# Source order on every engine through the mixer and the attention of a hybrid decoder layer

## The chip, the cores and the metric

The kernel runs on one core of one Trainium2 chip. The metric is the device time of one execution in microseconds (us), from 3 runs of the kernel before: 849.39, 850.27 and 852.31, median 850.27. A core has five engines with a queue each: TensorE (PE in the profile, with its weight loads as PEld), VectorE (DVE), ScalarE (ACT), GpSimd (POOL) and SyncE (SP). The compiled program gives each engine a list of instructions in a fixed order; semaphores order the engines among each other. SP and POOL also issue the DMAs.

## The reference

One decoder layer in f32 over 512 positions of width 1024:

- RMSNorm, then one projection whose columns are cut into two head groups. The HGRN2 group (4 heads of 128) is a gated linear recurrence, computed in chunks of 32 positions: forget gates through a sigmoid, running products of them, a masked product inside a chunk, states from chunk to chunk, an RMSNorm per head and a swish gate. The MoBA group (4 heads of 128) is causal attention with partial rotary. With 512 positions there are two blocks of 256, so all past blocks are chosen and the result is plain causal softmax attention.
- The outputs of both groups side by side go through the output projection; residual add.
- RMSNorm, then cross-attention with 4 heads of 256 into 256 memory tokens, which have an RMSNorm of their own; residual add.
- RMSNorm, an MLP of width 4096 with the square of relu; residual add; a final RMSNorm.

```python
h = rms_norm(x, norm_mix);  hq, hf, hi, hg, mq, mk, mv = split(h @ w_in)
x = x + concat([hgrn2_mixer(hq, hf, hi, hg, ...), moba_attention(rot(mq), rot(mk), mv)]) @ w_out
x = x + cross_attention(rms_norm(x, norm_xattn), rms_norm(mem, norm_mem), w_xq, w_xk, w_xv, w_xo)
x = x + square(relu(rms_norm(x, norm_mlp) @ w_ff1)) @ w_ff2
return rms_norm(x, norm_final)
```

## The kernel before

**Numbers in two parts.** Every f32 operand of a large product is split in a high part in fp32r (ACT: a copy, `wh`) and a low part (DVE: a subtraction, `wl`). A product is three matmuls: high by high, high by low, low by high. The MLP's two products use a Strassen-like scheme with seven block products in place of eight.

**Units.** The weights are cut into units of 128 x 1024 f32 (512 KB). A unit of a projection is eight k steps of three matmuls of 512 columns, 24 matmuls; a unit of `memk` has 24 of 256 columns, one of `memv` 12 of 512. The mixer and the cross-attention are units 0 to 67, in this order: `hf` 4 units, `hi` 4, `hq` 4, `mv` 4, `mkq` 8 (keys and queries of MoBA in turn), `hg` 4, `wo` 8 (output projection), `memk` 8, `xq` 8, `memv` 8, `xo` 8. Then comes the MLP.

**Loads and splits.** `need(u)`, called ahead of the matmuls of unit u, emits the work for later units: the split of unit u+2 (`SPLIT_AHEAD`) and the load of about unit u+5, since at most three raw tiles wait for their split (`RAWS`; four in the MLP). There are four tiles for high and four for low parts (`WBUFS`). Each load also emits one or two DMAs of the sums of weight blocks that the Strassen scheme wants (`more_sums`): copies from DRAM to DRAM on SP's queue (line 202) and accumulating DMAs on POOL's queue (line 205). Each of these waits for the last matmul of an earlier unit.

**Side work.** Between the matmuls of the units stands side work: the HGRN heads (`hgrn_pre`, `hgrn_out`), the MoBA heads (`moba_head`), the norms, the preparation of the memory (`mem_prep`) and the heads of the cross-attention (`xattn_probs`, `xattn_out`). Each is a Python generator that is started by the evacuation of a unit and yields where it wants to wait. Counted in the source, `hgrn_out` has 7 steps with PE work per head, `moba_head` 10, the cross-attention 10; with four heads each that is 28 + 40 + 40 = 108.

**The planner.** `Pace` keeps an estimate of when each tile is ready, from costs written into `note`: PE runs strictly in the order of emission; DVE, ACT, POOL and the DMAs take an instruction into the first gap that is long enough. After at least `GAP` = 4 matmuls `pump` emits the next step of the first piece of side work whose inputs are ready, by the planner, `SLACK` = 2.5 us before PE's planned time. `drain` emits all that is left of a piece at once, where the next unit cannot do without it. All instructions go through the planner's call at line 115, so nearly all rows of the profile have L115.

**What sets the order.** The compiler has a scheduler of its own: outside a region that the kernel marks as ordered it chooses the order of each engine's instructions at compile time, by a simulated run with its own costs. Inside a region opened by `tc.manual_schedule()` each engine issues its instructions in the order in which the source emits them. The kernel before has two such regions: from the start to `lower_bounds()` behind `hf`'s third unit (closed at line 565), and from the MLP's first group (opened at line 1155) to the end. Between them, from unit 3 through `xo`, the scheduler orders. The kernel's last line of the layer, 1248, closes the second region.

**Memory.** PSUM has four banks for the accumulators of the units and four for side work (`side_bank`). SBUF has 12 large tiles (`s8`, 128 x 2048 f32), 14 small ones (`s2`, 128 x 512) and 8 more small ones for the mixer (`e2`).

Of the kernel before, what the change touches and what calls it, by code (L numbers as in the profile page):

```python
# [122 lines left out]
def hybrid_layer(ctx: ExitStack, tc: tile.TileContext, xT, memT, ws, vecs, consts, rots, out):  # L123
# [12 lines left out]
    ordered = tc.manual_schedule()  # L136
# [144 lines left out]
    def need(u):  # L281
        marks.append(last_mm[0])
        want_load, want_split = min(UNITS, u + LOAD_AHEAD + 1), min(UNITS, u + SPLIT_AHEAD + 1)
        while state["split"] < want_split or state["load"] < want_load:
            if state["load"] < want_load and state["load"] - state["split"] < RAWS + (u >= MLP):
                load_unit()
            elif state["split"] < want_split:
                split_unit()
            else:
                break  # L290
# [244 lines left out]
    def lower_bounds():  # L535
        l0, l1 = vec[:, V_LB:V_LB + 4], vec[:, V_LB + 4:V_LB + 8]
        V.tensor_max(lb, l0, l1)
        V.tensor_sub(le0, l0, lb)
        V.tensor_sub(le1, l1, lb)
        A.activation(lbv[:, 2:4, :], lbv[:, 2:4, :], AF.Exp)  # L540
        V.tensor_add(le1, le0, le1)
        V.reciprocal(le1, le1)
        V.tensor_mul(lb, le0, le1)
        V.tensor_scalar(oml, lb, -1.0, 1.0, op0=ALU.mult, op1=ALU.add)
# [17 lines left out]
        if k == NORM_AT:  # L562
            next(norm_x)
    lower_bounds()
    ordered.__exit__(None, None, None)
    need(3)
    for k in range(KT):
        fm_k(3, accs[3], x_act, k, k == 0, k == KT - 1)
# [583 lines left out]
        while op_state[0] < min(28, i + 1):  # L1152
            make_op()

    ordered = tc.manual_schedule()
    ordered.__enter__()
    for j in range(8):
        f1_group(j)
        u += 7
# [163 lines left out]
```

## Time and profile before

| | |
|---|---|
| median of 3 runs | 850.27 us (849.39 to 852.31) |
| the profiled execution | 853.37 us, its span 851.4 us, 2.0 us outside of it |
| mean granted TensorE clock | 0.954 |
| PE busy | 768.0 us, 90% of the span |
| DVE busy | 536.2 us, 63% |
| ACT busy | 412.2 us, 48% |
| POOL busy | 89.8 us, 11% |
| DMA | 165.87 MB, mean 195 GB/s |

The span runs from the first to the last instruction; the rest of an execution's time lies around it. "Idle before, releaser" in a row names the engine and tile that ended a wait. Tiles carry their names without numbers: `wh<-wr` is the high part of some unit's weights, `mkq<-xhi,wl` a matmul of the stage `mkq` with the low part of a unit's weights. The granted clock is the share of its full rate that the throttle left to TensorE.

### The profile page before, as it was taken

What the parts mean: (1) busy time and instruction counts of PE and PEld (TensorE: products, weight loads), DVE (VectorE), ACT (ScalarE), POOL (GpSimd) and SP (SyncE); (2) the same over time, 40 slices, a digit from 0 to 9 for tenths busy, and PEclk for the clock granted to TensorE, in tenths of its full rate; (3) what the DMA queues carried; (4) which work ended last, traced back from release to release, by engine and by line L of the source; (5) the groups of instructions that cost most, each with busy time, mean ns of one, the idle gap of its engine ahead of it and who ended that gap; (6) DMA issues with size and microseconds to landing.
All of it is one profiled execution on the core that took longest, in us unless ns stands there. A gap on an engine that the chain in (4) does not pass through costs nothing.

```text
span 851.4 us, 12049 instructions
## 1 busy us (share of the span) xinstructions
PE 768.0 (90%) x4696; PEld 680.1 (80%) x4696; DVE 536.2 (63%) x854; ACT 412.2 (48%) x633; POOL 89.8 (11%) x99
## 2 busy tenths in 40 slices
PE   6998769669997796799999999999999999999994
PEld 3787647447775686788888899999999899989994
DVE  6896540346754276447655775667676767867783
ACT  6652472022453255434445566555555654455662
POOL 5140002101001021100131001100000000110011
PEclk9999979878998997899999999999999999998998
DMA  7443219958518969995699569986555565995641
GB/s 243 155 143 123 75 34 295 192 97 222 149 50 207 317 179 302 243 355 200 168 264 269 164 216 258 246 268 190 185 184 179 168 200 168 242 261 157 211 161 50
DMA packets 57481, 165.87 MB, mean 195 GB/s; under 512 B 5424, under 2 KB 7856, under 8 KB 56656
## 3 DMA queue, kind: packets, MB, share of 16 engines
q1 hardware_dynamic: 43632, 131.09, 45.0%
q0 software_dynamic: 13312, 33.56, 21.9%
q8 instruction: 37, 0.61, 0.3%
q10 hardware_dynamic: 480, 0.45, 0.2%
q14 instruction: 20, 0.16, 0.1%
HBM read 162.98 MB, written 65.01 MB: 268 GB/s over the span
## 4 chain that ended last, share of the span: by engine, by line
PE 54%; issue 18%; DVE 13%; ACT 6%; DMA 6%; POOL 1%; SPq 0%; POOLq 0%; ACTq 0%; DVEq 0%
PE X L115 9%; PE xo L115 6%; PE mkq L115 6%; PE Y L115 5%; PE xq L115 5%; DVE wl L115 4%; PE memk L115 3%; PE wo L115 3%; PE mv L115 3%; PE hg L115 3%; PE memv L115 3%; DMA mraw<-in_memT_dram 2%; ACT wh L115 2%; PE hq L115 2%; ACT L115 2%
## 5 line engine op out<-in xcount | busy, mean ns | idle before, releaser
L115 DVE TENSOR_TENSOR wl<-wr,wh 128x1024 fp32r<-128x1024 f32 (+1 forms) x179 | 214.9, 1213 | 123.8 <-ACT wh L115 117.2
L115 ACT ACTIVATE wh<-wr 128x1024 fp32r<-128x1024 f32 (+2 forms) x182 | 185.3, 1040 | 112.1 <-DMA wr<-in_ws_dram 48.6
L115 PE MATMUL X<-op,wh 128*128 128x256 f32 x512 | 97.8, 292 | 4.0 <-DVE op L115 1.2
L115 PEld LDWEIGHTS X<-op,wh 128*128 128x128 f32 x512 | 83.4, 200 | 5.2 <-DVE op L115 1.6
L115 PE MATMUL X<-op,wl 128*128 128x256 f32 x256 | 74.8, 292 | 1.5 <-DVE wl L115 1.5
L205 POOL DMA_DIRECT2D uf<-in_ws_dram x32 | 26.2, 872 | 386.8 <-PE X L115 190.3
L115 PEld LDWEIGHTS X<-op,wl 128*128 128x128 f32 x256 | 51.0, 199 | 2.2 <-DVE wl L115 2.1
L205 POOL DMA_DIRECT2D ue<-in_ws_dram x32 | 28.8, 1000 | 227.0 <-PE mv L115 75.7
L115 PE MATMUL Y<-op,wh 128*128 128x256 f32 x256 | 46.7, 284 | 0.6 <-DVE op L115 0.6
L115 PE MATMUL X<-OS,wh 128*128 128x256 f32 x256 | 47.0, 283 | 0.0
L115 PE MATMUL Y<-OS,wh 128*128 128x256 f32 x256 | 46.8, 283 | 0.0
L115 ACT ACTIVATE op<-g 128x1024 fp32r<-128x1024 f32 x28 | 29.4, 1050 | 34.5 <-DVE g L115 34.5
L115 ACT ACTIVATE g<-t 128x512 f32<-128x512 f32 x32 | 19.4, 628 | 55.0 <-DVE t L115 54.9
L115 DVE TENSOR_TENSOR op<-g,op 128x1024 fp32r<-128x1024 f32 x28 | 34.2, 1222 | 16.7 <-ACT op L115 16.7
L115 PEld LDWEIGHTS Y<-op,wh 128*128 128x128 f32 x256 | 40.0, 192 | 1.0 <-DVE op L115 1.0
L115 PEld LDWEIGHTS X<-OS,wh 128*128 128x128 f32 x256 | 40.0, 192 | 0.0
L115 PEld LDWEIGHTS Y<-OS,wh 128*128 128x128 f32 x256 | 39.9, 192 | 0.0
L115 PE MATMUL X<-OS,wl 128*128 128x256 f32 x128 | 36.3, 284 | 0.6 <-DVE wl L115 0.6
L115 PE MATMUL Y<-OS,wl 128*128 128x256 f32 x128 | 36.2, 283 | 0.0
L115 PE MATMUL Y<-op,wl 128*128 128x256 f32 x128 | 36.2, 283 | 0.0
L115 PE MATMUL wo<-mixhi,wh 128*128 128x512 f32 x64 | 27.3, 427 | 9.6 <-DVE x L115 4.9
L115 PE MATMUL mkq<-xhi,wl 128*128 128x512 f32 x64 | 28.4, 444 | 4.8 <-DVE wl L115 4.8
(298 smaller groups left out, 2022.8 us busy)
## 6 DMA issues: line engine op xcount, KB each, us to landing
wr<-in_ws_dram SPq DMA_DIRECT2D x114, 512.0 KB, 5.3
ue<-in_ws_dram POOLq DMA_DIRECT2D x32, 512.0 KB, 10.4
uf<-in_ws_dram POOLq DMA_DIRECT2D x32, 512.0 KB, 9.4
wr<-ue SPq DMA_DIRECT2D x32, 512.0 KB, 4.2
wr<-uf SPq DMA_DIRECT2D x32, 512.0 KB, 4.4
ue<-in_ws_dram SPq DMA_DIRECT2D x16, 512.0 KB, 6.5
ue<-ue SPq DMA_DIRECT2D x16, 512.0 KB, 7.0
uf<-in_ws_dram SPq DMA_DIRECT2D x16, 512.0 KB, 6.5
```

Source lines behind the costliest of these rows:

```text
L115: return f(*args, **kw)
L205: return nc.gpsimd.dma_start(dst, src, accum_op=ALU.add, max_dma_last_dim=4 * D)
```

## The change

The two lines that close the first ordered region and open the second are removed. One region then reaches from the start of the kernel to its end, and every engine issues every instruction in the order of the source. No instruction is added or taken away by the source; tiles, buffers, `need`, `pump`, `drain` and the planner's costs stay as they are.

```diff
         if k == NORM_AT:
             next(norm_x)
     lower_bounds()
-    ordered.__exit__(None, None, None)
     need(3)
     for k in range(KT):
         fm_k(3, accs[3], x_act, k, k == 0, k == KT - 1)
...
         while op_state[0] < min(28, i + 1):
             make_op()
 
-    ordered = tc.manual_schedule()
-    ordered.__enter__()
     for j in range(8):
         f1_group(j)
         u += 7
```

## The prediction

> **What bounds the kernel now.** I read the page first, then a table of busy time by stage, then the waits of TensorE in the stages that lose time, then the order of instructions around those waits.
>
> ```profile
> span 851.4 us, 12049 instructions
> PE 768.0 (90%) x4696; PEld 680.1 (80%) x4696; DVE 536.2 (63%) x854; ACT 412.2 (48%) x633; POOL 89.8 (11%) x99
> ```
>
> TensorE is the busiest engine; the others have room on the mean. The stages say more. The rows below are the mixer's first half (`hi`, `hq`, `mv` and HGRN's side work), its second half (`mkq`, `hg`, MoBA), `wo` and `memk`, then `xq`, `memv`, `xo`. The MLP's 349 us behind them keep their order.
>
> ```profile
> core 0: us, PE busy (x) PEld busy (x) DVE busy (x) ACT busy (x) POOL busy (x), PEclk, DMA share, GB/s
> 36.00:148.00 112.00, 94.80 (x462) 77.07 (x460) 61.11 (x157) 52.64 (x73) 15.30 (x14) 0.95 0.44 135
> 148.00:260.00 112.00, 96.06 (x386) 72.33 (x387) 64.05 (x139) 38.40 (x74) 10.35 (x12) 0.91 0.60 142
> 260.00:364.00 104.00, 82.28 (x401) 70.11 (x400) 53.18 (x71) 44.96 (x64) 17.67 (x18) 0.85 0.92 257
> 364.00:502.00 138.00, 138.00 (x678) 115.51 (x677) 89.48 (x174) 67.73 (x137) 13.16 (x16) 1.00 0.78 229
> ```
>
> These four rows are the region that changes hands. In their first three TensorE is idle for 17.2 + 15.9 + 21.7 = 54.9 us (length less PE busy). The granted clock is below 1 in the same rows and 1.00 where there is no idle time, so the idle time also costs clock. As an estimate, taking a row's mean clock for its busy part: 94.80 x 0.05 + 96.06 x 0.09 + 82.28 x 0.15 = 4.7 + 8.6 + 12.3 = 25.7 us. Together 80.6 us could go; from 364 to 502 there is nothing to win. The waits of TensorE from 36 to 364:
>
> ```profile
> engine line waited for: us in total, times, longest us
> PE pt L115 <- DVE pn L115: 5.1, 2, 4.9
> PE wo L115 <- DVE x L115: 4.9, 1, 4.9
> PE mkq L115 <- DVE wl L115: 4.8, 2, 4.2
> PE wo L115 <- ACT wh L115: 4.6, 1, 4.6
> PE memk L115 <- ACT wh L115: 3.8, 2, 1.9
> PE on L115 <- ACT osh L115: 3.7, 2, 3.0
> PE mv L115 <- ACT wh L115: 3.7, 1, 3.7
> PE sc L115 <- DVE z L115: 3.6, 1, 3.6
> PE mkq L115 <- ACT wh L115: 3.0, 2, 1.7
> PE hq L115 <- DVE wl L115: 2.8, 2, 1.7
> ...
> PE memk L115 <- DVE wl L115: 1.5, 2, 0.8
> ```
>
> There are two kinds. Waits for split weights (`wh`, `wl`): 4.8 + 4.6 + 3.8 + 3.7 + 3.0 + 2.8 + 1.5 = 24.2 us. The rest, 54.9 - 24.2 = 30.7 us, are waits of side work in the middle of its own chain.
>
> **Part 1: the weights' waits.** The scheduler put splits late though their data was there. ACT, then SP's loads:
>
> ```profile
> 119.93 1.28 ACT L115 ACT_TABLE_LOAD   x1
> 121.22 0.63 ACT L115 ACTIVATE osq<-osq 128x512 f32<-128x512 f32 x1
> 121.76 2.94 ACT L115 ACTIVATE wh<-wr 128x1024 fp32r<-128x1024 f32 x3
> ```
> ```profile
> 73.51 0.37 SPq L115 DMA_DIRECT2D wr<-in_ws_dram  x1
> 96.32 0.33 SPq L115 DMA_DIRECT2D wr<-in_ws_dram  x1
> 124.08 0.33 SPq L115 DMA_DIRECT2D wr<-in_ws_dram  x1
> ```
>
> Three splits ran together at 121.76, behind HGRN's last norm, and `mv` waited 3.7 us for the first. No load was issued between 96.32 and 124.08, because the raw tiles hung on those splits. On DVE the same:
>
> ```profile
> 155.73 0.69 DVE L115 TENSOR_TENSOR z<-mkq,rb 128x512 f32<-128x512 f32 x1 [5.38 <-PE mkq L115]
> ...
> 159.13 1.21 DVE L115 TENSOR_TENSOR wl<-wr,wh 128x1024 fp32r<-128x1024 f32 x1
> ```
>
> A `wl` stands behind the evacuation of a unit, for which DVE sat idle 5.38 us, and TensorE lost 4.2 us. In source order a split stands ahead of the matmuls of the unit two before it. What covers it is two units:
>
> ```profile
> 450.56 49.12 PE xo L115 x216
> ```
>
> 49.12 / 216 = 0.2274 us a matmul, so 5.46 us a unit and 10.9 us for two, against 2.94 / 3 = 0.98 us on ACT and 1.21 us on DVE for a split. A load stands right behind a split three units earlier, so the loads no longer come in lumps; every DMA on SP's queue keeps its place relative to them. I take these waits as gone except `memk`'s 3.8 + 1.5 us, whose units are half as long: -18.9 us (ends: 0 and -24.2).
>
> **Part 2: the chains' waits.** Where the scheduler's run went well, its order on TensorE is already the source's: one step, four matmuls, one step. From the chain that ended last:
>
> ```profile
> 205.09 0.93 PE mkq L115 x4
> 206.02 1.50 PE po L115 x4
> 207.52 0.93 PE mkq L115 x4
> ```
>
> This pattern holds around 204 to 260 and in `xq`, and the row 364 to 502 has no idle time at all. Elsewhere the steps are pushed together, and the first half has HGRN's chains beside `hq` while `mv` runs nearly bare. Spread by `pump`, with the planner's 2.5 us, the chains should wait as little as they do in the good stretches. They will not all do so: `drain` still forces a chain out, and the planner lets DVE fill gaps that an ordered DVE must leave. I take two thirds: -20.5 us (ends: 0, and -30.7). For new waits where there are none now, I add 3 us; the lower end is 0, the upper the rate of the bad rows on the good ones, 30.7 / 328 x 138 = 13 us.
>
> **Part 3: the clock.** Idle time kept is 54.9 - 18.9 - 20.5 + 3 = 18.5 us. The clock costs 25.7 / 54.9 = 0.47 us per idle us now, so 8.7 us then: -17.0 us (it moves with the other two).
>
> **Part 4: what the DMA gives back.** The third row keeps the 16 DMA engines at 0.92 for 104 us: 95.7 us of work. By parts 1 to 3 it would shrink to 82.28 - 12.3 + 9.2 idle + 4.3 clock = 83.5 us. The loads may run only some units ahead, so part of the missing 12.2 us returns as waits for loads, with these prices:
>
> ```profile
> q1 hardware_dynamic: 43632, 131.09, 45.0%
> q0 software_dynamic: 13312, 33.56, 21.9%
> ...
> wr<-in_ws_dram SPq DMA_DIRECT2D x114, 512.0 KB, 5.3
> ue<-in_ws_dram POOLq DMA_DIRECT2D x32, 512.0 KB, 10.4
> mraw<-in_memT_dram SPq DMA_DIRECT2D x1, 1024.0 KB, 17.6
> ```
>
> The 64 accumulating DMAs of q0 take 0.219 x 851.4 / 64 = 2.9 us of all engines each; 0.5 MB on q1 takes 0.45 x 851.4 x 0.524 / 131.09 = 1.5 us. The sums can slip, as only the MLP reads them, and the neighbours' shares are 0.60 and 0.78; so +7 us, between 0 and 12. The memory's load is in this sum too: ACT's and DVE's splits of it now stand a planned 6 us behind its issue and it took 17.6 us to land. What queues behind them on ACT are the evacuations of `wo` and the splits of units 35 and 36; the two split units (10.9 us) cover most of the 11.6 us.
>
> **The sum.** -18.9 - 20.5 + 3 - 17.0 + 7 = -46.4 us. The profiled execution took 853.4 us, so 807.0; it was 3.1 us above the median of 850.27, so **804 us**. The MLP and the start keep their order; nothing is booked there.
>
> **Rivals.**
>
> *The DMA holds more back.* The first half gains its 16.6 us (6.5 + 7.1 + 3.0 of the clock), the second, where the accumulating DMAs begin, half of its 20.5 us, the third row nothing, and the fourth loses 4.4 us: 22.4 us, 828 us. For it: the share of 0.92, and 17.6 us for one load. Against it: part of these queues is the lumps themselves. [...] The trace has q0's transfers land in 10.4 us against 5.3 us for the loads, but no run so far separates what one queue does to the other.
>
> *It recovers all but the DMA's floor.* 21.9 + 24.5 us in the first two rows, 104 - 95.7 = 8.3 us in the third: 54.7 us, 796 us; without that floor 770 us.
>
> *Slower: TensorE stalls at the fixed places of the side work.* An ordered TensorE can't go on with the next unit when a step's input is late, and the source has 108 such steps. With 5.3 us kept for weights and w us of waits on the mean per step, the loss is 1.47 x (5.3 + 108 w) against 80.6 us now; it decides from w = 0.46 us. At 0.65 us, two steps in five with 1.6 us, it is 110.5 us: 880 us. For it: DVE's chains through ACT leave holes the planner fills. Against it: those holes are small,
>
> ```profile
> DVE rs L115 <- ACT pn L115: 6.3, 12, 0.9
> ```
>
> half a us each, and the good stretches run with w near 0. [...]
>
> *No change.* The scheduler's order is the source's so widely that little moves, within 0.3% (2.6 us, about what a measurement of this kernel can tell): 850 us. Against it: the lumps at 121.76.
>
> **Chances.** Forecast, 788 to 822 us: 0.52. DMA rival, 822 to 847: 0.20. Better than 788: 0.08. No change: 0.05. Slower, from 853 up: 0.15. So faster 0.80, same 0.05, slower 0.15. The range 780 to 856 leaves out some 0.04 below and 0.12 above.
>
> **What would show it.** Part 1: splits singly, one per unit from `hi` to `xo`, two units ahead, and PE's waits for `wh` and `wl` near 5 us outside the MLP. Part 2: `ho`, `a` and `pd` spread over `mv` and `mkq`, DVE busier in `mv`, and less than 15 us of chain waits. Part 3: a granted clock above 0.95 in the first three rows. Part 4: `memk` still near a DMA share of 1, the wait for `mraw` on ACT. Wrong if side steps wait more than 0.46 us each, if `xq` to `xo` grow by more than 10 us, or if ACT stands at a load while TensorE is idle.

## The result and the profile after

The kernel after takes 827.73 us (median of 4 runs, 824.73 to 829.6) beside 850.06 us for the kernel before (4 runs): a ratio of 0.973, 95% interval 0.9692 to 0.9767. It is faster, as forecast, but by 22.3 us where 46.4 were forecast. The time lies inside the outer range of 780 to 856 us, outside the forecast's own 788 to 822, and in the DMA rival's 822 to 847. The profiled execution took 829.6 us, of which 827.6 are its span. From the page of the kernel after:

```profile
span 827.6 us, 12043 instructions
PE 753.3 (91%) x4696; PEld 668.8 (81%) x4696; DVE 539.8 (65%) x854; ACT 413.0 (50%) x633; POOL 95.2 (12%) x99
```

TensorE, DVE, ACT and POOL have as many instructions as before, and TensorE's busy time fell by 768.0 - 753.3 = 14.7 us with the same 4696 matmuls. Most of that is clock, as an estimate: the mean granted clock rose from 0.954 to 0.970, and 768.0 x 0.954 = 732.7 is close to 753.3 x 0.970 = 730.7. Busy time of the kernel after by stretch, cut where TensorE goes from one region to the next; the last row is the MLP's first 14 us:

```profile
core 0: us, PE busy (x) PEld busy (x) DVE busy (x) ACT busy (x) POOL busy (x), PEclk, DMA share, GB/s
36.00:131.40 95.40, 90.48 (x459) 76.41 (x460) 64.33 (x156) 50.95 (x70) 20.37 (x13) 0.96 0.65 191
131.40:224.00 92.60, 89.46 (x396) 68.50 (x395) 66.53 (x141) 41.66 (x78) 10.65 (x12) 1.00 0.69 166
224.00:322.20 98.20, 72.34 (x394) 62.42 (x393) 46.20 (x67) 41.45 (x58) 17.64 (x18) 0.88 0.82 221
322.20:466.30 144.10, 138.63 (x658) 112.02 (x657) 87.82 (x168) 65.53 (x131) 13.19 (x16) 1.00 0.83 240
466.30:480.00 13.70, 7.78 (x45) 6.70 (x44) 9.66 (x15) 7.52 (x12) 0.00 (x0) 0.88 0.36 116
```

The same cuts of the kernel before:

```profile
core 0: us, PE busy (x) PEld busy (x) DVE busy (x) ACT busy (x) POOL busy (x), PEclk, DMA share, GB/s
36.50:149.10 112.60, 94.43 (x460) 77.07 (x460) 60.61 (x155) 53.24 (x75) 16.40 (x15) 0.95 0.44 135
149.10:266.30 117.20, 97.75 (x392) 73.36 (x392) 67.58 (x145) 39.55 (x76) 11.04 (x13) 0.90 0.59 137
266.30:363.90 97.60, 80.49 (x393) 68.98 (x394) 49.65 (x66) 42.61 (x60) 15.88 (x16) 0.85 0.95 269
363.90:499.50 135.60, 135.60 (x658) 113.12 (x657) 88.01 (x170) 66.27 (x134) 13.16 (x16) 1.00 0.77 225
```

I call the four regions A (`hi`, `hq`, `mv`), B (`mkq`, `hg`), C (`wo`, `memk`) and D (`xq`, `memv`, `xo`). They are cut at the stages' first matmuls, up to 6.3 us from the round times of the prediction's four rows. Their lengths, and the MLP's, read from the first matmul of each stage, with all kernels that were run (medians and ratios are of timed runs, each ratio against the runs of the kernel before on the same chip; their medians were 850.06, 850.01, 849.02 and 848.9 us, so that a difference of 1 us between kernels of different rows says nothing. The lengths are of one profiled execution each; that of the kernel before was 3 us above its median):

| kernel | median us | ratio, 95% interval | A | B | C | D | MLP |
|---|---|---|---|---|---|---|---|
| before | 850.06 | | 112.6 | 117.1 | 97.6 | 135.6 | 351.9 |
| after | 827.73 | 0.973, 0.9692 to 0.9767 | 95.0 | 92.6 | 98.2 | 144.1 | 361.3 |
| e1_norm_later | 819.63 | 0.9642, 0.9616 to 0.9669 | 95.2 | 92.6 | 90.0 | 143.8 | 359.6 |
| e2_mem_later | 810.84 | 0.9526, 0.9494 to 0.9557 | 95.7 | 92.6 | 80.0 | 144.0 | 360.2 |
| e3_mixer_only | 815.30 | 0.9587, 0.9556 to 0.9619 | 94.9 | 85.8 | 110.9 | 135.8 | 347.4 |
| e4_attention_only | 875.29 | 1.0292, 1.0263 to 1.0322 | 112.3 | 119.3 | 103.7 | 143.7 | 357.6 |
| e5_xq_free | 800.13 | 0.9418, 0.9392 to 0.9443 | 94.4 | 92.6 | 80.3 | 142.3 | 349.7 |
| e6_xo_order | 803.11 | 0.9456, 0.9431 to 0.9482 | 95.3 | 92.6 | 81.2 | 143.7 | 351.0 |
| e7_f_order | 807.04 | 0.9516, 0.9474 to 0.9559 | 91.7 | 92.6 | 79.9 | 143.8 | 357.7 |
| e8_sums_moved | 824.80 | 0.9717, 0.9685 to 0.9749 | 95.1 | 92.6 | 92.2 | 147.8 | 360.1 |
| e9_both_orders | 800.13 | 0.942, 0.9389 to 0.9451 | 91.1 | 92.6 | 81.6 | 143.9 | 353.6 |
| e10_load_free | 798.34 | 0.9406, 0.9367 to 0.9445 | 91.7 | 92.6 | 76.5 | 147.7 | 350.2 |
| e11_all | 805.44 | 0.9484, 0.9449 to 0.9519 | 91.2 | 92.6 | 77.7 | 156.1 | 349.2 |
| e12_before_edits | 840.24 | 0.9907, 0.9875 to 0.9939 | 113.4 | 117.7 | 87.3 | 135.9 | 348.3 |

Between before and after, A gained 17.6 us and B 24.5, C gained nothing, D lost 8.5 and the MLP 9.4. TensorE's waits in the kernel after, from `hi` to the MLP's first 14 us (the tiles X and Y are the MLP's):

```profile
engine line waited for: us in total, times, longest us
PE nr L115 <- ACT nrh L115: 23.5, 2, 22.2
PE xt L115 <- DVE xp L115: 4.6, 7, 1.9
PE Y L115 <- ACT wh L115: 2.9, 1, 2.9
PE hi L115 <- DVE wl L115: 2.3, 1, 2.3
PE hi L115 <- ACT wh L115: 2.1, 1, 2.1
PE po L115 <- ACT PT L115: 1.4, 1, 1.4
PE memk L115 <- DVE wl L115: 1.2, 2, 0.8
PE sc L115 <- DVE z L115: 1.1, 1, 1.1
```

One wait of 22.2 us stands out: the column sums `nr` of the memory's norm, which the source puts between two matmuls of `wo`. In order of time on TensorE, with the idle time before the instruction and its releaser in brackets:

```profile
243.25 0.39 PE L115 MATMUL wo<-mixlo,wh 128*128 128x512 f32 x1
265.85 0.58 PE L115 MATMUL nr<-nrh,ones_r 128*128 128x256 f32 x1 [22.22 <-ACT nrh L115]
```

The chain of waits of the kernel after at this place (start, length, what; the splits and evacuations of `wo` between are left out):

```profile
230.78 15.02 DMA mraw<-in_memT_dram
...
245.82 0.52 ACT mhi L115
...
258.99 1.81 ACT msq L115
...
260.87 2.33 POOL msq L115
...
263.29 1.26 POOL msq L115
...
264.63 0.73 POOL Sm L115
265.38 0.42 ACT nrh L115
...
265.85 1.04 PE nr L115 x2
```

The memory's load was issued at 230.78 us and landed 15.0 us later; the planner had booked 6.0. On ACT, which now keeps the source's order, the load's first user stood in the queue from the time ACT was free:

```profile
228.03 1.99 ACT L115 ACTIVATE wh<-wr 128x1024 fp32r<-128x1024 f32 x2
245.82 0.51 ACT L115 ACTIVATE mhi<-mraw,vec 128x256 fp32r<-128x256 f32 x1 [15.80 <-DMA mraw<-in_memT_dram]
```

For 15.8 us ACT did none of `wo`'s evacuations and weights' splits behind it. They came out afterwards among the memory's own splits, so from landing to the end of the sums on POOL another 19.6 us went by (245.80 to 265.36). The clock at this wait:

```profile
248.20:265.80 17.60, 0.00 (x0) 0.00 (x0) 9.97 (x16) 9.98 (x17) 4.77 (x4) 0.50 0.49 130
265.80:272.00 6.20, 6.15 (x15) 4.82 (x16) 1.12 (x2) 3.54 (x5) 1.27 (x2) 0.50 0.89 137
```

The clock was at half for most of the wait, where no matmul ran, and for 6.2 us beyond it, about 3 us of work lost. So the mean of 0.88 in C's row makes the clock look dearer than it was: TensorE's busy time in C fell from 80.49 to 72.34 us.

At the MLP's start the waits are shorter and more. The last row of the table of stretches has 13.70 - 7.78 = 5.9 us of idle time in 14 us, at a clock of 0.88. What is late there is the end of `xo`. VectorE in the kernel after, over the evacuation of two units:

```profile
459.24 0.68 DVE L115 TENSOR_TENSOR x<-xo,x 128x512 f32<-128x512 f32 x1
461.23 0.69 DVE L115 TENSOR_TENSOR S<-S,sq 128x512 f32<-128x512 f32 x1 [1.31 <-ACT sq L115]
...
464.64 1.22 DVE L115 TENSOR_TENSOR OS<-xs,OS 128x1024 fp32r<-128x1024 f32 x1 [1.13 <-ACT OS L115]
...
471.91 0.68 DVE L115 TENSOR_TENSOR x<-xo,x 128x512 f32<-128x512 f32 x1
```

DVE and ACT hand the tile to each other call by call, in the order in which the source writes the calls down, and each waits for the other (up to 480 us ACT waits 9.4 us in all for DVE's `xs`, in four waits). A pair of units takes 471.91 - 459.24 = 12.67 us this way, against 10.9 us of matmuls for two units, so the evacuation falls behind from pair to pair. That TensorE meets this delay where the MLP needs the result is what e6_xo_order tests.

### The profile page after: what moved, and what is told of

Read it like the earlier page. It is cut to its first block, busy times and chain, and to the rows that moved or that the text cites. A ratio compares the mean times of both kernels' runs of the same rounds, so it can differ in the third digit from the quotient of the medians.

```text
span 827.6 us, 12043 instructions
## 1 busy us (share of the span) xinstructions
PE 753.3 (91%) x4696; PEld 668.8 (81%) x4696; DVE 539.8 (65%) x854; ACT 413.0 (50%) x633; POOL 95.2 (12%) x99
## 4 chain that ended last, share of the span: by engine, by line
PE 33%; DVE 23%; issue 21%; ACT 13%; DMA 7%; POOL 2%; POOLq 0%; SPq 0%; ACTq 0%; DVEq 0%
PE X L115 10%; DVE wl L115 7%; PE Y L115 6%; ACT wh L115 4%; DMA wr<-in_ws_dram 4%; PE wo L115 3%; PE mv L115 3%; PE hq L115 3%; PE mkq L115 2%; PE xq L115 2%; DMA mraw<-in_memT_dram 2%; DVE t L115 1%; ACT pn L115 1%; PE a L115 1%; DVE z L115 1%
## 5 line engine op out<-in xcount | busy, mean ns | idle before, releaser
L205 POOL DMA_DIRECT2D uf<-in_ws_dram x32 | 26.2, 873 | 394.6 <-PE X L115 197.2
L115 DVE TENSOR_TENSOR op<-g,op 128x1024 fp32r<-128x1024 f32 x28 | 34.2, 1222 | 16.7 <-ACT op L115 16.7
L115 PE MATMUL X<-OA,wh 128*128 128x256 f32 x128 | 25.2, 295 | 1.6 <-ACT OA L115 1.1
```

Source lines behind the costliest of these rows:

```text
L115: return f(*args, **kw)
L205: return nc.gpsimd.dma_start(dst, src, accum_op=ALU.add, max_dma_last_dim=4 * D)
```

## Experiments

Theory P says that the two losses, C and the MLP's start, come from source order kept on ACT and DVE at places where the source's order rests on too short a time for the load or makes the two engines take turns. Theory D says that the faster mixer has the DMA engines to pay for, and that C to the MLP would be slow in any order.

**e1_norm_later.** The memory norm's column sums are given a fixed 16 us from the end of the sums by the planner, in place of the planned end alone; on TensorE they stand 71 instructions later.

```diff
         PO.tensor_add(S[:, :M], sq[:, :M], sq[:, M:2 * M])
-        yield [S[:, :M]]
+        yield 16.0
         yield from norm_rows(S, M, rbm, rcm)
```

> The changed kernel, with only the memory norm's last steps (TensorE's column sums and what feeds them) planned 16 us later, so that they stand some 71 matmuls later in wo. Theory P (the order gains 42 us in the mixer and gives some 34 us back in one place, TensorE standing 22.2 us at the memory norm, whose load lands 15.0 us after its issue where 6 us were planned, with the clock at half for 24 us): the wait goes, the half clock mostly; what is late next is the split of unit 36, which stands on ACT behind the memory's splits and costs 6 to 8 us: 800 to 810 us. Theory D (the DMA engines bind wo and memk, as in the rival at 828 us): the wait turns up at another matmul and the time stays at 822 to 830 us.

Measured: 819.63 us, between the two expectations, and C 8.2 us shorter. The wait came apart, in `wo` and at the norm:

```profile
PE wo L115 <- ACT wh L115: 7.4, 1, 7.4
PE nr L115 <- ACT nrh L115: 5.7, 2, 4.5
```

The norm's place on TensorE is worth 8 us by itself. With the norm out of the way, TensorE waits 7.4 us for a weights' split that stands behind the memory's splits on ACT: the load holds ACT, and ACT holds `wo`.

**e2_mem_later.** The memory's splits are put 12 us behind the issue of the load instead of 6, and the norm 12 us behind its sums.

```diff
         SY.dma_start(mraw, memT)
-        yield 6.0
+        yield 12.0
...
         PO.tensor_add(S[:, :M], sq[:, :M], sq[:, M:2 * M])
-        yield [S[:, :M]]
+        yield 12.0
         yield from norm_rows(S, M, rbm, rcm)
```

> The changed kernel, with the memory's splits planned 12 us instead of 6 us behind the issue of its load and the memory norm 12 us behind them. Theory P: ACT and DVE no longer stand at the load, so unit 36's split is not late either: 792 to 802 us, and a clock of 1.00 in wo. Theory D: 822 to 830 us, with waits for wh and wl in wo and memk.

Measured: 810.84 us, 16.9 us under the kernel after, C 80.0 us instead of 98.2. With two numbers of the planner's hints changed, C is 17.6 us shorter than in the kernel before, where 13.5 were forecast. Theory D's 822 to 830 is out. It is short of P's 792 to 802, for one wait of 6.4 us is left at `nr`, and the MLP's start is as it was. What holds `nr` here is seen on DVE:

```profile
258.38 0.68 DVE L115 TENSOR_TENSOR x<-wo,xr 128x512 f32<-128x512 f32 x1
263.69 0.75 DVE L115 SCALAR_TENSOR_TENSOR x1lo<-x,vec,x1hi 128x512 fp32r<-128x512 f32 x1 [4.64 <-POOL Sm L115]
```

An evacuation of `wo` writes `x1lo`, and it waits for the memory's sums on POOL, with which it has no data in common. A reading of it is that `x1lo` and the memory's squares are both among the 12 large tiles, and that the buffer is free only when the sums have been taken; no run shows that it is the buffer. The chain of waits goes on from this `x1lo` through the next evacuation of `wo` on DVE (266.18 us), its `x1hi` and `sq` and a `wh` on ACT (266.81 to 269.01 us) to DVE's `nrl` at 270.18 us and the `nr` behind it at 270.65 us.

**e3_mixer_only and e4_attention_only.** Source order through `hg` alone, with the scheduler from `wo` to `xo` as before; and the other half alone.

```diff
     fm_stage(u, x_act, T, ev_g, "hg", ONE * 4)
     u += 4
+    ordered.__exit__(None, None, None)
...
+    ordered = tc.manual_schedule()
+    ordered.__enter__()
     for j in range(8):
         f1_group(j)
```
```diff
     lower_bounds()
+    ordered.__exit__(None, None, None)
     need(3)
...
     fm_stage(u, x_act, T, ev_g, "hg", ONE * 4)
     u += 4
+    ordered = tc.manual_schedule()
+    ordered.__enter__()
```

> Source order through hg, the scheduler's from wo through xo, source order in the MLP. Theory P (stages add up): the mixer's 42 us are all there, and wo to the MLP's start are as before: 806 to 814 us. Theory D (a faster mixer only moves the DMA's load into wo): wo and memk grow past the 98 us of before, 820 to 835 us.

> The scheduler's order through hg, source order from wo to the end. Theory P: wo and memk about even, xq to xo 8 us and the MLP's start 9 us longer, as in the changed kernel: 862 to 872 us, with TensorE's long wait at the memory norm. Theory D (the long wait comes of the faster mixer's DMA traffic): no such wait, 845 to 855 us.

Measured: 815.30 and 875.29 us, 1 and 3 us above Theory P's ranges. Source order in the mixer is a gain of 35 us by itself (A and B are 49 us shorter, C 13 us longer, in part because some 20 of B's matmuls stand in C there); in the attention it is a loss of 25 us, with the mixer as slow as before. The long wait came here too, so it needs no faster mixer, which speaks against D. The wait of the second kernel:

```profile
PE nr L115 <- ACT nrh L115: 24.6, 1, 24.6
```

The first shows what the scheduler makes of C when the mixer is faster. Its longest there:

```profile
PE memk L115 <- DVE x L115: 19.1, 2, 14.8
```

C grew to 110.9 us, past the 98 of before as Theory D had it for this kernel; the longest of it is a wait for an evacuation of `wo`. So the scheduler is no cure for this place either.

**e8_sums_moved.** The kernel after, without the accumulating and copying DMAs of the weights' sums that are issued with the loads 34 to 39; one more goes with each of the loads 40 to 49.

```diff
         if u < MLP:
             n, it = 2 - (u % 3 == 0), first_sums
+            if 34 <= u < 40:
+                n = 0
+            elif 40 <= u < 50:
+                n += 1
```

> The changed kernel, with no sums issued with the loads 34 to 39 and one more with each of the loads 40 to 49: the memory's load no longer has five accumulating DMAs beside it. Theory P and D agree that the landing is late because of these: it lands in 7 to 9 us instead of 15.0, TensorE's 22.2 us at the memory norm become 13 to 16 us, the whole 814 to 822 us. If the landing stays at 14 us or more, the load is slow for another reason (its own 1 MB and the loads beside it).

Measured: 824.80 us, 2.9 us under the kernel after; its interval, 0.9685 to 0.9749, overlaps that of the kernel after, so the time alone settles nothing, and the expectation missed. The trace does settle what it was made for. The memory's load and the wait for the norm:

```profile
mraw<-in_memT_dram SPq DMA_DIRECT2D x1, 1024.0 KB, 8.9
```
```profile
PE nr L115 <- ACT nrh L115: 17.3, 2, 16.1
```

Against 15.0 us and 22.2 us in the kernel after: the load is 6.1 us shorter, the wait 6.1 us shorter, C 6.0 us shorter. The sums beside the load made 6.1 us of its 15.0, and through it 6.1 us of the wait. D then grew by 3.7 us: the sums that were put off go with the loads 40 to 49, and in `xq` TensorE waits 2.2 us for `wh` and 1.1 us for `wl`, where the kernel after has no such wait.

**e5_xq_free and e6_xo_order.** Both start from e2_mem_later. The first gives `xq` to `xo` back to the scheduler. The second keeps source order and writes down the same calls of `xo`'s evacuation in another order: the splits of `a`, which need no other engine's answer, fill the time in which DVE's four differences run.

```diff
     drain("n2")
+    ordered.__exit__(None, None, None)
...
+    ordered = tc.manual_schedule()
+    ordered.__enter__()
     for j in range(8):
         f1_group(j)
```
```diff
         A.activation(q, dst, AF.Square)
-        if j:
-            V.tensor_add(S2, S2, q)
...
             A.activation(hi, a[:, :half], AF.Copy)
+            if j:
+                V.tensor_add(S2, S2, q)
...
+        bhi, blo = s2(F32R, f"OBh{k}"), s2(F32R, f"OBl{k}")
+        OB.append((bhi, blo))
+        A.activation(bhi, a, AF.Copy)
         A.activation(hi, raw, AF.Copy)
+        V.tensor_sub(blo, a, bhi.bitcast(F32))
+        V.tensor_add(S2, S2, q)
         V.tensor_sub(lo, raw, hi.bitcast(F32))
         OS.append((hi, lo))
-        hi, lo = s2(F32R, f"OBh{k}"), s2(F32R, f"OBl{k}")
-        OB.append((hi, lo))
-        A.activation(hi, a, AF.Copy)
-        V.tensor_sub(lo, a, hi.bitcast(F32))
```

> The kernel of e2_mem_later, with the region closed ahead of xq and opened again at the MLP, so that the scheduler orders xq, memv and xo as it did before. Theory P (stages add up; in xq to xo and at the MLP's start source order costs 8.5 + 9 us, since DVE and ACT wait for each other inside the evacuations): 790 to 797 us, xq to xo near 136 us, the MLP near 350 us. Theory D (the faster front makes the DMA engines bind behind it, whatever the order): 805 to 813 us.

> The kernel of e2_mem_later, with the instructions of xo's evacuation in another order in the source: the sum of squares and the low half of OB are put where DVE would wait for ACT. The same instructions. Theory P (DVE's holes of 1.31, 2.35 on ACT and 1.13 us per pair of units make a pair take 12.7 us against the 10.9 us of its matmuls, so the evacuation reaches the MLP's start some 5 us late, plus half clock): the MLP's stretch falls from 360 to 351 to 354 us, the whole to 801 to 806 us. Theory D: the waits at the MLP's start are for loads, no change within 2 us.

Measured: 800.13 and 803.11 us; the first is 3 us above Theory P's range, since D did not come near 136, the second is inside it. In both the gain is the MLP's: 360.2 us went to 349.7 and to 351.0; D stays at 142.3 and 143.7. So the order of calls in one evacuation is worth 9.2 us here, nearly all of the 9.4 that the MLP lost. (In e9_both_orders, with the same edit, the MLP takes 353.6 us.) DVE over two units of `xo`, in the kernel with the calls reordered:

```profile
438.34 0.68 DVE L115 TENSOR_TENSOR x<-xo,x 128x512 f32<-128x512 f32 x1
439.81 0.42 DVE L115 TENSOR_TENSOR xs<-xa,xa 128x256 f32<-128x256 f32 x1 [0.79 <-ACT xa L115]
...
449.30 0.69 DVE L115 TENSOR_TENSOR x<-xo,x 128x512 f32<-128x512 f32 x1
```

A pair takes 449.30 - 438.34 = 10.96 us, which is what the matmuls take. D's own 8 us are not explained by either theory: the scheduler got back 1.7 of them here.

**e7_f_order.** From e2_mem_later; the evacuation behind `hf` runs in three loops over the heads, so that ACT has four sigmoids in one piece and DVE does not wait between them.

```diff
     for h in range(HEADS):
-        ev_f(h, accs[h])
+        V.tensor_mul(Fz[:, h, :], accs[h], rb1)
+    for h in range(HEADS):
+        A.activation(Fz[:, h, :], Fz[:, h, :], AF.Sigmoid)
+    for h in range(HEADS):
+        V.tensor_scalar(Fz[:, h, :], Fz[:, h, :], oml[:, h:h + 1], lb[:, h:h + 1], op0=ALU.mult, op1=ALU.add)
```

> The kernel of e2_mem_later, with the evacuation of hf in three loops over the heads (all products, all sigmoids, all scalings) in place of one head after the other. The same instructions. Theory P: hi, which is 31 us against 23 us before, gets back 4 to 8 us; the whole 802 to 808 us. Rival: hi is long because the chains of hgrn_pre are in front of the splits on DVE, and the order inside the evacuation is worth under 2 us.

Measured: 807.04 us, 3.8 us under e2_mem_later by the medians, with ratios that overlap (0.9516 and 0.9526), so the time leaves it open. In the trace A is 4.0 us shorter: `hi` went from 31.1 to 25.4 us, its waits for `wh` and `wl` are gone, and 2.3 us came back as a wait in `hq`. One of the sigmoids in the kernel after, and the four in this one:

```profile
38.10 0.63 ACT L115 ACTIVATE Fz<-Fz 128x512 f32<-128x512 f32 x1 [1.21 <-DVE Fz L115]
```
```profile
36.64 2.43 ACT L115 ACTIVATE Fz<-Fz 128x512 f32<-128x512 f32 x4 [0.78 <-DVE Fz L115]
```

**e9_both_orders, e10_load_free, e11_all.** The first has the edits of e2_mem_later, e6_xo_order and e7_f_order together. The second adds sums kept off the memory's load and the time booked for it. The third adds the scheduler for `xq` to `xo`, as in e5_xq_free.

```diff
             n, it = 2 - (u % 3 == 0), first_sums
+            if 34 <= u < 39:
+                n = 0
+            elif 50 <= u < 59:
+                n += 1
...
         SY.dma_start(mraw, memT)
-        yield 12.0
+        yield 9.0
```

> The kernel of the change with the later memory norm (810.8 us) and both rewritten evacuations: the one behind xo (7.7 us less by itself) and the one behind hi (3.8 us less by itself). Theory P, the calls' order inside an evacuation is the price of source order and the two places are independent: 810.8 - 7.7 - 3.8 = 799, so 797 to 802. Theory D, what one saves the DMA queues take back from the other: 803 to 808.

> The same with no sums of weights issued with the loads 34 to 38 (nine fewer) and one more with each of the loads 50 to 58, so that the memory's load has the DMA engines to itself, and with 9.0 us booked for that load in place of 12.0. Theory P: the 6.4 us that TensorE waits at the memory norm's column sums come from the load (14.9 us) by way of GpSimd's sums of squares, which end at 263.65 us and hold the buffer that VectorE's next x1lo needs; with the load down in about 9 us they end some 5 us sooner, that wait and its half clock (6.8 us at half) go, and the time is 790 to 795. Theory D, the sums that were put off are paid for later: the wait goes, but xq to xo grow by 4 us or more, 796 to 802. If the wait stays at 5 us or more, the load was not what held it.

> The same with the scheduler's order for xq to xo. By Theory P the scheduler gains there only what the rewritten evacuation behind xo has not gained already: the kernel with the later norm went from 810.8 to 800.1 by the scheduler and to 803.1 by the rewritten evacuation, so 3 us are left: 787 to 792, or 3 us under the run without it. If the scheduler's order is better in all of xq to xo for other reasons, 5 to 10 us under it. If source order is as good there, 1 us or less.

Measured: 800.13, 798.34 and 805.44 us. The first agrees with P: the two evacuations' gains add up (10.7 us under e2_mem_later, against 7.7 + 3.8). In the second the load took 7.0 us, VectorE's wait of 4.6 us for the memory's sums is gone, and the one wait of 6.4 us at `nr` has become two, the longer of 3.0 us:

```profile
PE nr L115 <- ACT nrh L115: 4.3, 2, 3.0
```

C went from 81.6 to 76.5 us, but D grew by 3.8, close to the 4 us that Theory D had for this run, so the time lies within 2 us of e9_both_orders, with overlapping intervals, and P's 790 to 795 was missed. These two and e5_xq_free (800.13) are the fastest kernels run.

The third went against all its expectations. With the scheduler, D takes 156.1 us where e5_xq_free had 142.3, nearly all in `xq`. That stage, first in e10_load_free, then in e11_all:

```profile
296.90:358.30 61.40, 57.51 (x288) 47.20 (x287) 35.11 (x78) 24.32 (x58) 4.42 (x5) 0.97 0.98 298
```
```profile
297.60:371.80 74.20, 64.24 (x289) 51.20 (x288) 36.10 (x82) 25.06 (x62) 4.41 (x5) 0.88 0.83 252
```

Same work, 10.0 us of idle time in place of 3.9, and a clock of 0.88. In D the scheduler gained 1.7 us in one kernel and lost 8.4 us in the other, most of it in `xq`, whose code is the same in both. What comes before it, the sums beside it and the calls of `xo`'s evacuation differ; which of them it was, no run shows.

**e12_before_edits.** The kernel before, scheduler and all, with the three edits of e9_both_orders.

> The kernel before, with the scheduler's order, and with the three edits that were made to the changed one: the later memory norm and both rewritten evacuations. Theory P, in the scheduler's order the place of a call in the source decides little, and these edits repair what only source order breaks: 846 to 853, the kernel before within 0.5%. Theory E, the edits are gains of their own which would have come without the change: 25 us less as in the changed kernel, 823 to 830.

Measured: 840.24 us, between the two expectations. About a third of what the edits bring to the changed kernel (27.6 us) they bring here as well (8.7 us), mostly in C, which fell from 97.6 to 87.3 us. So they are not only repairs. Between this kernel and e9_both_orders, with the same edits in both, source order is worth 840.24 - 800.13 = 40.1 us.

## Why the prediction was right and wrong

By region the prediction had 16.6 + 20.5 + 13.5 - 4.4 + 0 = 46.2 us (A, B, C, D, MLP), and 17.6 + 24.5 - 0.6 - 8.5 - 9.4 = 23.6 us came. What is missing is 14.1 us in C, 9.4 in the MLP and 4.1 in D; A and B gave 5.0 more.

**Parts 1 and 2, the weights' and the chains' waits: right in A and B.** Regions A and B were to gain 16.6 and 20.5 us; they gained 17.6 and 24.5. Outside the MLP, waits for `wh` and `wl` above 1 us are 2.3 + 2.1 + 1.2 = 5.6 us, where 5.3 were kept; but 4.4 of them lie in `hi`, where e7_f_order removes them, and not in `memk`. The side work spread as part 2 said: in `mv` TensorE had 96 matmuls in 26.2 us and now has 194 in 34.2 us without idle time, and DVE 36 instructions in place of 4. With the norm's column sums left aside, chain waits above 1 us are 4.6 + 1.4 + 1.1 = 7.1 us, under the 15 asked for; with them (23.5) they are 30.6 us, twice what was allowed, so this sign failed in C. One reading was loose: of the 30.7 us called chain waits, 4.9 + 2.2 = 7.1 were `wo` and `memk` waiting for an evacuation (`x`), not for side work.

**Part 3, the clock: right in size.** In A and B it stood at 0.96 and 1.00, above the 0.95 asked for; in C at 0.88, under it, since the wait stayed. But most of that half clock fell into the wait. TensorE's busy time in A to C fell from 94.43 + 97.75 + 80.49 = 272.67 to 90.48 + 89.46 + 72.34 = 252.28 us, by 20.4 us for nearly the same matmuls, where 17.0 were booked. What failed in C is the idle time: 9.2 us were kept for it, and it grew from 17.1 to 25.9.

**Part 4, the memory's load: the step that failed.** The text said that behind the load on ACT stood `wo`'s evacuations and the splits of units 35 and 36, and that "the two split units (10.9 us) cover most of the 11.6 us". Three things were wrong in it.
- The list of what queues behind was not followed to TensorE. The memory norm's column sums stand in TensorE's own queue, in the middle of `wo`, at the planned time; no split unit covers them. TensorE stopped at 243.6 us with more than half of `wo` to do (224.0 to 243.6 us is 19.6 us, 3.6 units of 5.46 us out of eight).
- Only the load's own lateness was priced. ACT stood at the load from 230.0 to 245.8 us, and TensorE stopped at 243.6: only 2.2 of the 22.2 us of its wait lie before the landing. Once the load has landed, ACT has the queued evacuations and splits to do in between, and POOL's three sums take 2.33 + 1.26 + 0.73 = 4.3 us: 15.0 us of load were followed by 20 us of chain.
- The loss was mixed up with the DMA engines' share of time. The 95.7 us of DMA work were no floor. In e2_mem_later, which moves no DMA in the source, C is this row, 80.0 us at a share of 0.94, about 75 us of work; part of the rest is done in A and D, where the shares went from 0.44 to 0.65 and from 0.77 to 0.83 with the change. What is shown of the DMA engines holding C came by way of one load.

```profile
224.70:304.70 80.00, 71.16 (x393) 61.34 (x392) 45.57 (x67) 41.23 (x58) 17.74 (x18) 0.96 0.94 268
```

C was to gain 13.5 us net and lost 0.6. e2_mem_later takes 18.2 us off C by two of the planner's numbers, and e8_sums_moved shows the sums' share, 6.1 us of the 22.2.

**"The MLP and the start keep their order; nothing is booked there": failed by 9.4 us.** The MLP's order was kept, but not the time at which its inputs are ready. `xo`'s evacuation was looked at as a place with no idle time on TensorE, with no look at whether the calls written in its function, run in that order on two engines, fit into the time of a unit: 12.67 us against 10.9 for a pair. e6_xo_order has 9.2 of the 9.4 us back with the same instructions.

**The 3 us for new waits where there were none:** D was to lose 4.4 us with the clock and lost 8.5. 4.6 us of it are the `xt` waits and 0.9 us other idle time; the last 3.0 us are longer busy time for the same 658 matmuls at a clock of 1.00. What makes these was not settled, and neither the scheduler (142.3 us) nor the reordered evacuation (143.7) removed it.

**The rivals.** The one of the DMA engines had 828 us, and the kernel takes 827.7. That agreement is luck, for its parts do not fit: B was to gain half and gained more than all; the MLP's 9.4 us were not in it; C was to gain nothing and did, but from one load and from source order behind it. What POOL's accumulations do to a load on SP's queue, which no run had separated until then, e8_sums_moved shows for the memory's: in the kernel after, four of them were issued in the 6.3 us ahead of this load and one 4.5 us behind it; without them it took 8.9 us instead of 15.0. The prediction's last sentence, that it is wrong "if ACT stands at a load while TensorE is idle", names what happened, 15.8 us in one row, though most of TensorE's wait came after it.

The rival of side steps that stall at each of 108 places failed: idle time in A, B and D is 4.9 + 3.1 + 5.5 = 13.5 us, where 0.46 us a step would make 49.7. Yet its mechanism, an ordered TensorE that cannot pass a late step, is what cost 22.2 us at a single step, the memory norm's, which is not among the 108.

With the two failed steps repaired (e9_both_orders), source order gains 40.1 us over the scheduler's order with the same edits; the forecast of 46 is near that in its sum and not by region (A and B gain 22.2 and 25.1 us between these two kernels, C 5.7, and D and the MLP lose 8.0 and 5.3). It missed that two places would have to be made fit for source order.

## What to carry to other kernels

Before an engine's order is fixed by the source, go through its queues once for the places where a cross-engine step depends on a booked time: a load whose landing time the trace shows to be longer than booked, and all that stands behind its first user on that engine and, through it, on TensorE. Then go through each evacuation as written: if DVE and ACT answer each other call by call, add up the round, not the busy time, and compare it with the time of a unit. For the first the trace of before had the numbers, 17.6 us to land where 6.0 were booked; the second takes the source beside it. Both were cheap to mend: two planner numbers and a few moved lines.

## What was not expected of the hardware

- The 1 MB load took 15.0 us, 8.9 us and 7.0 us in three kernels: in the first with five accumulating DMAs of 0.5 MB issued between 6.3 us ahead of it and 4.5 us behind it, in the other two these five were put off. The same load took about twice as long with these neighbours, and moving them moved part of the price into D, which grew by 3.7 and 3.8 us.
- One wait of 22.2 us kept the clock at half for only 6.2 us of the work behind it, about 3 us lost. In the kernel before, 54.9 us of idle time in many small waits went with some 25.7 us of clock by the prediction's estimate, of which 20.4 us of busy time are gone after the change. In these two profiles the one long wait cost the clock less for each us of idle time than the many short ones.
